# Hybrid decoder trunk on one core: query/key projections with 512 moving columns, distance tables on ScalarE and VectorE, and two dense pieces per step early in attention

## The chip, the cores and the metric

The kernel runs on one core of a Trainium2 chip. The metric is the device time of one execution in microseconds (us). Engines are named as the profile names them: PE is TensorE's matmul, PEld its weight load, DVE is VectorE, ACT is ScalarE, POOL is GpSimd, SP is SyncE (here it issues the weight DMAs).

## The reference

Two layers of a decoder trunk with 256 positions and width 1024, then a final RMS norm. Each layer normalises x, projects it with one wide matrix, runs three causal token mixers side by side, gates and sums them, and adds a SwiGLU feed-forward block:

```python
h = _rms_norm(x, attn_norm)
aq, ak, av, bq, bk, bv, c_q, c_kv_pe, gates = jnp.split(h @ w_in, offsets, axis=-1)
y_a = _diff_attention(aq, ak, av, ...) @ w_branch_a       # 4 heads x 2 maps of 64, distance slopes
y_b = _dilated_attention(bq, bk, bv, slopes_b) @ w_branch_b   # 4 heads of 128, three strides
y_c = _mla(c_q, c_kv_pe, ...) @ w_branch_c                # 8 heads, latent q and kv, rope
g_a, g_b, g_c = jnp.split(jax.nn.sigmoid(gates), 3, axis=-1)
x = x + (g_a * y_a + g_b * y_b + g_c * y_c) @ w_out
h2 = _rms_norm(x, ffn_norm)
x = x + (jax.nn.silu(h2 @ w_ffn_gate) * (h2 @ w_ffn_up)) @ w_ffn_down
```

All inputs are float32.

## The kernel before

**Numbers in two parts.** A float32 matrix is held as two tiles of the matmul type fp32r: `hi`, a copy rounded by ACT (`hi_of`, line 223), and `lo`, the rest, by a DVE subtraction (`lo_of`, lines 228 and 230). A product is the sum of three matmuls, hi with hi, hi with lo and lo with hi (`mm3`, lines 212 to 215).

**Weights.** `PLAN` lists every weight block in order of use, in pieces of up to 1024 columns a partition. `dma_piece` (line 242) loads a piece into one of 5 `raw` tiles; `split_piece` makes `whi` on ACT and `wlo` on DVE, 5 tiles of each. `take` (line 255) hands out the next piece and splits a later one, 3 pieces ahead.

**The dense stream.** `dense` (line 455) is a generator of one layer's projections, which yields after each weight piece: the latent projections (8 pieces), query/key of mixer a (`qk_proj`, 8), the latent up-projections (`mla_up`, 5), values of a (4), query/key of b (8), values of b (4), and then for each of the branches a, c, b in turn two times a gate (4) and a branch product (2). `pump(n)` draws n pieces. 25 pieces are drawn ahead of `attention`, and there `pump(1)` (line 936) draws one at the end of each of 22 steps; what is left is drawn after it. The steps run the scores, softmax, transposes, values and outputs of 16 heads (4 of a, 8 of c, 4 of b) at fixed lags. The order that is written here is not yet the order on the engines: the Tile framework schedules the instructions of each engine at build time by a timeline of its own (`schedule_with_timeline_sim`), and an instruction written earlier goes first where both are ready. Each engine then runs its own list strictly in order.

**Query/key projections.** `qk_proj` (lines 505 to 527) has four jobs j, two for queries and two for keys, each for 256 output columns. A job takes one PSUM bank of four (`N_DENSE`), and `pair_job` (lines 263 to 273) fills it over 8 row blocks k and 2 column blocks c with the weights stationary and the activations x[k] moving. The tile x[k] holds 256 columns of hi and, beside them, 256 columns of lo, and each of the three matmuls of `mm3` moves 256 columns. Then DVE multiplies the bank by the norm factor of each position (line 514 or 516), the bank is free, and the result t is split into hi and lo on ACT and DVE (`stacked` for mixer a, lines 495 to 502; lines 522 and 525 for b).

**Distance tables.** `tables` (lines 326 to 345), called once in layer 0, loads three constants and makes 8 tables of 128x256 on POOL: 4 for a (line 338), 4 for b with two instructions each (lines 342 and 343). The softmax reads them (line 757). POOL's other work is the rope (lines 602 to 605), the reciprocal roots (line 372) and the scaling of a's outputs (line 843).

**Tiles.** `PairRing` holds 16 tiles (`N_PAIR`) of 1024 columns for split activations; each is used whole or as two halves.

Of the kernel before, what the change touches and what calls it, by code (L numbers as in the profile page):

```python
# [12 lines left out]
F32 = mybir.dt.float32  # L13
F32R = mybir.dt.float32r
AF = mybir.ActivationFunctionType
ALU = mybir.AluOpType
# [13 lines left out]
SLOPE_A = [2.0 ** -(2 * h + 1) for h in range(4)]  # L30
SLOPE_B = [2.0 ** -(2 * h + 2) for h in range(4)]
SL = (slice(256, 384), slice(0, 256))
MASKED = 3.0e32
PIECE = 1024
N_PAIR = 16
N_F = 9
N_DENSE = 4
N_RAW = 5
N_PIECE = 5
AHEAD = 3  # L40
LAG_T, LAG_V, LAG_O, LAG_X = 3, 4, 6, 2
WARM = 10

C_ID, C_DM, C_DB, C_LC, C_TC, C_CS = 0, 128, 384, 640, 896, 1152
# [130 lines left out]
def fields(t):  # L175
    v = t.rearrange("p (c f t) -> p c f t", c=2, f=2)
    return v[:, :, 0], v[:, :, 1]


def split_rows(t):  # L180
    return t.rearrange("p (c t) -> p c t", c=2)


class Build:
    def __init__(self, nc, tc, ctx, x, xt, w, gains, lam, fnorm, cst, out):
# [6 lines left out]
        def ring(n, cols, dt, name, pool=cp):  # L192
            return Ring([pool.tile([128, cols], dt, name=f"{name}{i}") for i in range(n)])

        self.banks = ring(N_DENSE, 512, F32, "bank", pp)
        self.att = ring(8 - N_DENSE, 512, F32, "att", pp)
        self.fr = PairRing([cp.tile([128, 1024], F32R, name=f"fr{i}") for i in range(N_PAIR)])
        self.f = ring(N_F, 512, F32, "f")
# [26 lines left out]
    def lo_of(self, lo, src, hi, scale=None):  # L225
# [3 lines left out]
        else:  # L229
            self.nc.vector.scalar_tensor_tensor(out=lo, in0=src, scalar=scale, in1=h, op0=ALU.mult, op1=ALU.subtract)  # L230

    def split(self, hi, lo, src, scale=None):
        self.hi_of(hi, src, 1.0 if scale is None else scale)
        self.lo_of(lo, src, hi, scale)
# [26 lines left out]
        return [(self.whi[j][:, k * nc_:(k + 1) * nc_], self.wlo[j][:, k * nc_:(k + 1) * nc_]) for k in range(nk)]  # L261

    def pair_job(self, ps, x, nk):
        k = 0
        while k < nk:
            for wh, wl in self.take():
                for c in range(2):
                    s = slice(c * 128, c * 128 + 128)
                    self.mm3(ps[:, c * 256:c * 256 + 256], wh[:, s], wl[:, s], x[k][:, 0:256], x[k][:, 256:512],
                             k == 0 and c == 0, k == nk - 1)  # L270
                k += 1
            if k < nk:
                yield
# [15 lines left out]
    def setup(self):  # L289
# [19 lines left out]
        bank = self.banks.get()  # L309
        for _ in range(WARM):  # L310
            self.mm(bank[:, 0:128], self.ones, self.ones, True, True)
# [14 lines left out]
    def tables(self):  # L326
        nc, cp = self.nc, self.cp
        dm, db = self.f.get(), self.f.get()
        nc.sync.dma_start(out=dm[:, 0:256], in_=self.cst_in[:, C_DM:C_DM + 256])
        nc.sync.dma_start(out=db, in_=self.cst_in[:, C_DB:C_DB + 512])  # L330
        self.tc_c = cp.tile([128, 256], F32, name="tcc")
        nc.sync.dma_start(out=self.tc_c, in_=self.cst_in[:, C_TC:C_TC + 256])
        self.cs = cp.tile([128, 2, 2, 32], F32, name="cs")
        nc.sync.dma_start(out=self.cs, in_=self.cst_in[:, C_CS:C_CS + 128].rearrange("p (f b c) -> p f b c", f=2, b=2))
        self.ta, self.tb = [], []
        for h in range(4):
            t = cp.tile([128, 256], F32, name=f"ta{h}")
            nc.gpsimd.tensor_scalar(out=t, in0=dm[:, 0:256], scalar1=SLOPE_A[h], scalar2=None, op0=ALU.mult)
            self.ta.append(t)
        for h in range(4):  # L340
            t = cp.tile([128, 256], F32, name=f"tb{h}")
            nc.gpsimd.tensor_scalar(out=t, in0=db[:, 0:256], scalar1=SLOPE_B[h], scalar2=None, op0=ALU.mult)
            nc.gpsimd.tensor_tensor(out=t, in0=t, in1=db[:, 256:512], op=ALU.subtract)
            self.tb.append(t)
        self.f.put(dm, db)

# [136 lines left out]
        yield from self.branch(self.oc, False, False)  # L483
        yield from self.branch(self.ob, False, True)

    def key_pair(self, src, rows=slice(0, 128)):
        kd = self.fr.pair()
        self.split(*fields(kd[rows]), src)
        return kd

    def stacked(self, t, query, j):
# [13 lines left out]
    def qk_proj(self, q, k, scale, stacked):  # L505
        nc = self.nc
        for j in range(4):
            bank = self.banks.get()
            yield from self.pair_job(bank, self.xs, KT)
            ps = split_rows(bank)  # L510
            t = self.f.get()
            tv = split_rows(t)
            if j < 2:
                nc.vector.scalar_tensor_tensor(out=tv, in0=ps, scalar=-scale, in1=self.Rb, op0=ALU.mult, op1=ALU.mult)
            else:
                nc.vector.tensor_tensor(out=tv, in0=ps, in1=self.Rb, op=ALU.mult)  # L516
            self.banks.put(bank)
            if stacked:
                (q if j < 2 else k).append(self.stacked(t, j < 2, j))
            elif j < 2:  # L520
                hi, lo = self.fr.get(), self.fr.get()
                self.split(hi, lo, t)
                q.append((hi, lo))
            else:
                k.append(self.key_pair(tv))
            self.f.put(t)
            yield
# [391 lines left out]
    def attention(self, l, pump):  # L919
        self.pairs = {}  # L920
        units = [("a", h) for h in range(4)] + [("c", h) for h in range(8)] + [("b", h) for h in range(4)]
        stages = [self.unit_stages(kind, l, h) for kind, h in units]
        n = len(stages)

        def run(i, stage):
            if 0 <= i < n and stages[i][stage] is not None:
                stages[i][stage]()

        for s in range(n + LAG_O):
            run(s, 1)  # L930
            run(s - LAG_T, 3)
            run(s - LAG_V, 4)
            run(s - LAG_O, 5)
            run(s + LAG_X, 0)
            run(s, 2)
            pump(1)


    def out_proj(self, pairs, nk, g0, late):
# [212 lines left out]
```

## Time and profile before

| | |
|---|---|
| median of 3 runs | 884.61 us (883.76 to 885.02) |
| the profiled execution's own time | 883.18 us |
| its span, first to last instruction | 881.4 us |
| granted TensorE clock, share of full speed | 0.999 |
| PE busy | 873.6 us (99%), 4710 matmuls |
| DVE busy | 591.1 us (67%) |
| ACT busy | 502.2 us (57%) |
| POOL busy | 71.4 us (8%) |
| weights and inputs read | 154.03 MB, 176 GB/s over the span |

In the profile a line number such as L210 is that of the code above, and a helper's line stands for everything that calls it: all matmuls are L210, so they are told apart by their tiles. In `bank<-fr,whi` the tile `bank` is written, `fr` (activations) moves and `whi` (weights) is stationary, or the other way round in `bank<-whi,fr`. Matmuls are pipelined: a matmul's own duration includes its way through the array, and the next one starts long before it ends. What one costs is the distance from its start to the start of the next.

### The profile page before, as it was taken

To read this page: it belongs to the slowest core of one execution; us is meant where nothing else is said; L and a number is where in the kernel's file an instruction comes from. 1 tells how busy PE (TensorE), PEld (TensorE's weight loads), DVE (VectorE), ACT (ScalarE), POOL (GpSimd) and SP (SyncE) were. 2 spreads that over 40 slices of the span, in tenths; PEclk is the share of its full clock that TensorE was granted. 3 is DMA by queue.
4 is the path that set the end of the run, shared out by engine and by line. 5 is a ranking of instruction groups with operands and counts; after the bars stand their busy time and mean duration, and the time that the engine had idled before them with its cause. 6 is when DMAs were issued, how large, how long until landed. Compare 5 with 4: busy or idle time off the path is not lost.

```text
span 881.4 us, 12736 instructions
## 1 busy us (share of the span) xinstructions
PE 873.6 (99%) x4710; PEld 759.5 (86%) x4710; DVE 591.1 (67%) x990; ACT 502.2 (57%) x852; POOL 71.4 (8%) x95
## 2 busy tenths in 40 slices
PE   9999999999999999999999999999999999999997
PEld 9989988888888888888899899888888888888886
DVE  5988878665666655555467888786556666656444
ACT  7797777644454444444376867775454644444332
POOL 1940310000000000000011303100000000000000
PEclk9999999999999999999999999999999999999999
DMA  9756444456656665656475553444555556655541
GB/s 340 245 170 209 128 141 160 146 169 193 187 167 197 187 190 182 182 186 191 127 226 174 172 168 128 151 145 159 180 189 182 167 193 202 203 190 180 181 141 49
DMA packets 45423, 155.92 MB, mean 177 GB/s; under 512 B 5168, under 2 KB 6192, under 8 KB 45360
## 3 DMA queue, kind: packets, MB, share of 16 engines
q1 hardware_dynamic: 44928, 154.55, 55.0%
q8 instruction: 37, 0.61, 0.3%
q10 hardware_dynamic: 432, 0.55, 0.2%
q14 instruction: 26, 0.21, 0.1%
HBM read 154.03 MB, written 1.05 MB: 176 GB/s over the span
## 4 chain that ended last, share of the span: by engine, by line
PE 97%; POOL 1%; issue 1%; DVE 0%; ACT 0%; POOLq 0%
PE bank L210 87%; PE att L210 6%; PE att L445 2%; PE att L719 1%; PE att L767 0%; PE att L768 0%; PE att L769 0%; POOL f L602 0%; PE att L693 0%; PE att L851 0%; POOL f L604 0%; POOL f L603 0%; POOL q_tm L605 0%; DVE x_tm L1043 0%; ACT x_tm L1058 0%
## 5 line engine op out<-in xcount | busy, mean ns | idle before, releaser
L210 PE MATMUL bank<-whi,fr 128*128 128x512 f32 (+1 forms) x2032 | 631.1, 387 | 0.0
L228 DVE TENSOR_TENSOR wlo<-raw,whi 128x1024 fp32r<-128x1024 f32 (+2 forms) x294 | 353.9, 1206 | 250.8 <-ACT whi L223 250.1
L223 ACT ACTIVATE whi<-raw 128x1024 fp32r<-128x1024 f32 (+2 forms) x294 | 305.0, 1041 | 305.8 <-PE bank L210 246.0
L210 PEld LDWEIGHTS bank<-whi,fr 128*128 128x128 f32 x2032 | 379.8, 188 | 71.5 <-ACT whi L223 0.2
L210 PE MATMUL bank<-wlo,fr 128*128 128x512 f32 (+1 forms) x1016 | 390.1, 386 | 0.0
L210 PEld LDWEIGHTS bank<-wlo,fr 128*128 128x128 f32 x1016 | 191.0, 188 | 35.5 <-DVE wlo L228 0.3
L210 PE MATMUL bank<-fr,whi 128*128 128x256 f32 x512 | 94.6, 285 | 0.0
L210 PEld LDWEIGHTS bank<-fr,whi 128*128 128x128 f32 x512 | 80.0, 192 | 0.2
L210 PE MATMUL bank<-fr,wlo 128*128 128x256 f32 x256 | 73.0, 285 | 0.0
L210 PEld LDWEIGHTS bank<-fr,wlo 128*128 128x128 f32 x256 | 49.0, 192 | 0.0
L372 POOL TENSOR_TENSOR r<-small,mhalf 128x2 f32<-128x2 f32 x4 | 2.8, 708 | 477.5 <-DVE small L398 462.6
L759 ACT ACTIVATE s<-s,small 128x256 f32<-128x256 f32 (+1 forms) x80 | 35.8, 455 | 1.2 <-DVE small L757 0.8
L372 POOL TENSOR_TENSOR small<-small,mhalf 128x2 f32<-128x2 f32 (+1 forms) x12 | 10.0, 831 | 280.5 <-DVE small L1047 178.5
L223 ACT ACTIVATE fr<-att 128x512 fp32r<-128x512 f32 (+2 forms) x54 | 28.3, 559 | 4.1 <-PE att L719 2.3
L210 PE MATMUL att<-whi,fr 128*128 128x288 f32 (+1 forms) x108 | 29.9, 290 | 0.0
L228 DVE TENSOR_TENSOR fr<-att,fr 128x512 fp32r<-128x512 f32 (+2 forms) x46 | 28.2, 634 | 0.1
L223 ACT ACTIVATE fr<-f 64x512 fp32r<-64x512 f32 (+2 forms) x40 | 23.3, 583 | 6.7 <-DVE f L516 5.4
L210 PE MATMUL att<-fr,fr 96*128 96x256 f32 (+3 forms) x152 | 26.0, 277 | 0.0
L210 PEld LDWEIGHTS att<-fr,fr 96*128 96x128 f32 (+1 forms) x152 | 22.7, 190 | 0.6
L615 ACT ACTIVATE f<-bank,rh 128x512 f32<-128x512 f32 x24 | 16.3, 689 | 11.7 <-PE bank L210 11.7
L972 ACT ACTIVATE f<-bank,rh 128x512 f32<-128x512 f32 (+1 forms) x24 | 15.6, 654 | 12.2 <-PE bank L210 12.2
L210 PEld LDWEIGHTS att<-whi,fr 128*128 128x128 f32 x108 | 20.4, 191 | 0.1
(134 smaller groups left out, 636.0 us busy)
## 6 DMA issues: line engine op xcount, KB each, us to landing
raw<-w SPq DMA_DIRECT2D x272, 512.0 KB, 3.6
raw<-w SPq DMA_DIRECT2D x16, 336.0 KB, 3.2
raw<-w SPq DMA_DIRECT2D x6, 384.0 KB, 3.6
x_tm<-xt SPq DMA_DIRECT2D x2, 512.0 KB, 6.4
f<-x SPq DMA_DIRECT2D x3, 256.0 KB, 5.2
f<-fnorm SPq DMA_DIRECT2D x2, 256.0 KB, 4.2
out<-x_tm ACTq DMA_DIRECT2D x2, 256.0 KB, 2.2
f<-x SPq DMA_DIRECT2D x2, 128.0 KB, 3.1
```

What stands on the lines that cost most here:

```text
L210: self.nc.tensor.matmul(out, lhsT, rhs, start=start, stop=stop, skip_group_check=True)
L223: self.nc.scalar.activation(out=hi, in_=src, func=AF.Copy, scale=scale)
L228: self.nc.vector.tensor_tensor(out=lo, in0=src, in1=h, op=ALU.subtract)
L372: self.nc.gpsimd.tensor_tensor(out=out, in0=v, in1=self.mhalf[:, 0:v.shape[1]], op=ALU.pow)
L445: self.nc.tensor.transpose(ps[:, c, b * 128:b * 128 + 128], src[b][:, c0 + c * 128:c0 + c * 128 + 128], self.ident)
L615: nc.scalar.activation(out=t[b], in_=bank[b], func=AF.Tanh, scale=self.rh[:, b:b + 1])
L719: nc.tensor.transpose(ps[0:96, c, b * 128:b * 128 + 128], src[:, b, 2 * p + c, :], self.ident)
L759: nc.scalar.activation(out=s[:, SL[b]], in_=s[:, SL[b]], func=AF.Exp, bias=mn[:, b:b + 1], scale=-1.0, accum_out=z[:, b:b + 1])
L972: nc.scalar.activation(out=a, in_=g, func=AF.Tanh, scale=self.rh[:, b:b + 1])
```

## The change

The query/key job takes two banks, one for each column block c. The stationary hi weights meet hi and lo of x[k] in one matmul of 512 moving columns, and the lo weights meet hi in one of 256 as before. To empty a bank, ACT copies its right half (with the scale of the queries), DVE adds the left half to it, and after both banks POOL multiplies by the norm factor; then t is split as before. `key_pair` and line 522 are written out, with the same instructions (`lo_pool` and the argument `pool` are not used by any call). The tables are made by ACT (a) and by one DVE instruction each (b). `attention` draws two pieces in the steps 0 to 7. There are 18 tiles in place of 16 in `PairRing`, and the SBUF set aside for DMA descriptors is cut to 1024 bytes a partition; no DMA of the profile was issued from POOL.

```diff
-N_PAIR = 16
+N_PAIR = 18
...
+SLOW = 8
...
+    def lo_pool(self, lo, src, hi):
+        self.nc.gpsimd.tensor_tensor(out=lo, in0=src, in1=hi.bitcast(F32), op=ALU.subtract)
...
     def pair_job(self, ps, x, nk):
...
                 for c in range(2):
                     s = slice(c * 128, c * 128 + 128)
-                    self.mm3(ps[:, c * 256:c * 256 + 256], wh[:, s], wl[:, s], x[k][:, 0:256], x[k][:, 256:512],
-                             k == 0 and c == 0, k == nk - 1)
+                    self.mm(ps[c], wh[:, s], x[k], k == 0, False)
+                    self.mm(ps[c][:, 0:256], wl[:, s], x[k][:, 0:256], False, k == nk - 1)
...
-            nc.gpsimd.tensor_scalar(out=t, in0=dm[:, 0:256], scalar1=SLOPE_A[h], scalar2=None, op0=ALU.mult)
+            nc.scalar.activation(out=t, in_=dm[:, 0:256], func=AF.Copy, scale=SLOPE_A[h])
...
-            nc.gpsimd.tensor_scalar(out=t, in0=db[:, 0:256], scalar1=SLOPE_B[h], scalar2=None, op0=ALU.mult)
-            nc.gpsimd.tensor_tensor(out=t, in0=t, in1=db[:, 256:512], op=ALU.subtract)
+            nc.vector.scalar_tensor_tensor(out=t, in0=db[:, 0:256], scalar=SLOPE_B[h], in1=db[:, 256:512], op0=ALU.mult,
+                                           op1=ALU.subtract)
...
-    def key_pair(self, src, rows=slice(0, 128)):
+    def key_pair(self, src, rows=slice(0, 128), pool=False):
         kd = self.fr.pair()
-        self.split(*fields(kd[rows]), src)
+        hi, lo = fields(kd[rows])
+        self.hi_of(hi, src)
+        (self.lo_pool if pool else self.lo_of)(lo, src, hi)
         return kd
...
         for j in range(4):
-            bank = self.banks.get()
+            bank = [self.banks.get() for _ in range(2)]
             yield from self.pair_job(bank, self.xs, KT)
-            ps = split_rows(bank)
             t = self.f.get()
             tv = split_rows(t)
-            if j < 2:
-                nc.vector.scalar_tensor_tensor(out=tv, in0=ps, scalar=-scale, in1=self.Rb, op0=ALU.mult, op1=ALU.mult)
-            else:
-                nc.vector.tensor_tensor(out=tv, in0=ps, in1=self.Rb, op=ALU.mult)
-            self.banks.put(bank)
+            sign = -scale if j < 2 else 1.0
+            for c in range(2):
+                nc.scalar.activation(out=tv[:, c], in_=bank[c][:, 256:512], func=AF.Copy, scale=sign)
+                nc.vector.scalar_tensor_tensor(out=tv[:, c], in0=bank[c][:, 0:256], scalar=sign, in1=tv[:, c],
+                                               op0=ALU.mult, op1=ALU.add)
+            self.banks.put(*bank)
+            nc.gpsimd.tensor_tensor(out=tv, in0=tv, in1=self.Rb, op=ALU.mult)
             if stacked:
                 (q if j < 2 else k).append(self.stacked(t, j < 2, j))
             elif j < 2:
                 hi, lo = self.fr.get(), self.fr.get()
-                self.split(hi, lo, t)
+                self.hi_of(hi, t)
+                self.lo_of(lo, t, hi)
                 q.append((hi, lo))
...
-            pump(1)
+            pump(2 if s < SLOW else 1)
...
-    nc = bacc.Bacc("TRN2", target_bir_lowering=False, num_devices=1)
+    nc = bacc.Bacc("TRN2", target_bir_lowering=False, num_devices=1, dynamic_dma_scratch_size=1024)
```

## Rows read from the trace of the kernel before

**Rows 1.** The page: span, busy time, and the chain that ended last

```profile
span 881.4 us, 12736 instructions
...
PE 873.6 (99%) x4710; PEld 759.5 (86%) x4710; DVE 591.1 (67%) x990; ACT 502.2 (57%) x852; POOL 71.4 (8%) x95
...
PE 97%; POOL 1%; issue 1%; DVE 0%; ACT 0%; POOLq 0%
```

**Rows 2.** Timeline of PE, 25 to 46 us: start, us, line, count

```profile
25.58 0.40 PE L210 MATMUL bank<-fr,whi 128*128 128x256 f32 x2
...
45.26 0.28 PE L210 MATMUL bank<-fr,wlo 128*128 128x256 f32 x1
```

**Rows 3.** Timeline of PE, 178 to 220 us: start, us, line, count

```profile
178.27 0.67 PE L210 MATMUL bank<-whi,fr 128*128 128x512 f32 x2
...
219.16 0.39 PE L210 MATMUL bank<-whi,fr 128*128 128x512 f32 x1
```

**Rows 4.** Groups by line and shape, PE: count | busy us, mean ns | idle

```profile
L210 PE MATMUL bank<-fr,whi 128*128 128x256 f32 x512 | 94.6, 285 | 0.0
L210 PE MATMUL bank<-fr,wlo 128*128 128x256 f32 x256 | 73.0, 285 | 0.0
```

**Rows 5.** Timeline, 59 to 61 us: the wait of the query transposes

```profile
59.78 0.28 PE L719 MATMUL att<-ident,q_tm 128*96 128x128 f32 x1
59.83 0.73 POOL L605 TENSOR_TENSOR q_tm<-f,f 128x256 f32<-128x256 f32 x1
...
60.62 0.54 PE L719 MATMUL att<-ident,q_tm 128*96 128x128 f32 x3 [0.55 <-POOL q_tm L605]
```

**Rows 6.** Groups by line and shape: what the new instructions resemble

```profile
L514 DVE SCALAR_TENSOR_TENSOR f<-bank,row 128x512 f32<-128x512 f32 x8 | 5.5, 687 | 2.0 <-PE bank L210 1.9
L588 ACT ACTIVATE k_tm<-bank,rk 128x256 f32<-128x256 f32 x8 | 3.9, 485 | 0.0
L230 DVE SCALAR_TENSOR_TENSOR fr<-att,gains,fr 128x256 fp32r<-128x256 f32 x34 | 14.6, 477 | 0.4 <-ACT fr L223 0.3
```

**Rows 7.** Timeline of POOL: tables (24 and 29 us), query rope (53 and 56)

```profile
24.23 4.49 POOL L338 TENSOR_SCALAR ta<-f 128x256 f32<-128x256 f32 x4
...
29.06 5.47 POOL L342 TENSOR_SCALAR tb<-f 128x256 f32<-128x256 f32 x4
...
52.86 0.75 POOL L602 TENSOR_TENSOR f<-q_tm,cs 128x256 f32<-128x256 f32 x1 [6.92 <-ACT q_tm L563]
...
56.21 1.72 POOL L602 TENSOR_TENSOR f<-q_tm,cs 128x256 f32<-128x256 f32 x1
```

**Rows 8.** Busy us (count) in stretches: PE, PEld, DVE, ACT, POOL; clock, DMA

```profile
21.00:33.00 12.00, 12.00 (x103) 11.97 (x102) 9.85 (x23) 12.00 (x28) 9.47 (x12) 1.00 0.80 279
33.00:45.30 12.30, 12.30 (x105) 12.30 (x104) 12.08 (x14) 5.69 (x10) 12.30 (x15) 1.00 0.69 225
45.30:60.00 14.70, 14.70 (x87) 13.62 (x86) 12.44 (x27) 14.54 (x29) 7.62 (x9) 1.00 0.57 174
60.00:80.00 20.00, 19.45 (x120) 17.50 (x120) 17.89 (x42) 15.66 (x35) 0.56 (x1) 1.00 0.66 210
80.00:100.00 20.00, 20.00 (x174) 20.00 (x173) 18.44 (x57) 15.21 (x40) 1.90 (x3) 1.00 0.50 143
456.00:470.00 14.00, 14.00 (x120) 14.00 (x119) 11.12 (x18) 11.33 (x25) 5.41 (x14) 1.00 0.60 187
470.00:482.00 12.00, 12.00 (x99) 12.00 (x98) 8.10 (x11) 7.81 (x11) 0.00 (x0) 1.00 0.49 161
```

**Rows 9.** Timeline of ACT, 39 to 45 us: a wait for DVE

```profile
39.02 0.85 ACT L223 ACTIVATE whi<-raw 128x768 fp32r<-128x768 f32 x1 [0.74 <-ACT fr L223]
44.60 0.64 ACT L223 ACTIVATE fr<-f 64x512 fp32r<-64x512 f32 x1 [4.73 <-DVE f L516]
```

**Rows 10.** Timeline of DVE: a weight split beside POOL, and one without

```profile
57.47 1.55 DVE L228 TENSOR_TENSOR wlo<-raw,whi 128x1024 fp32r<-128x1024 f32 x1
...
65.69 1.21 DVE L228 TENSOR_TENSOR wlo<-raw,whi 128x1024 fp32r<-128x1024 f32 x1
```

## The prediction

> **What bounds the kernel now.** I read the page first: PE is busy 99% of the span, and the chain that ended last is PE for 97% of it [rows 1]. A busy share is not yet a bound, because the matmuls overlap, so the next view is PE's timeline, where the distance between starts is the cost. In the first query/key projections 164 steps of 256 columns lie between 25.58 and 45.26 us: 19.68 us / 164 = 120.0 ns each [rows 2]. In a long stretch of 512 columns 180 steps take 40.89 us: 227.2 ns each [rows 3]. Both run without a break; PE is the bound through its own rate and not through waits. The one wait of PE that I found after the start-up, over 0.3 us, is at 60 us, where a transpose waits for POOL's rope of the queries: 0.84 us between the starts [rows 5]. A matmul of 128 columns costs at most the 0.12 us of 256, so 0.7 us are lost there. The last view is the busy time by stretch: around the first projections ACT and DVE are nearly full [rows 8]. That is where a change that gives them work can hurt.
>
> **Part 1, the matmuls.** There are 512 matmuls with the hi weights and 256 with the lo weights in the query/key jobs [rows 4], that is 256 triples of 3 x 120.0 = 360.0 ns. After the change each is one of 512 and one of 256 columns: 227.2 + 120.0 = 347.2 ns. The moved columns stay 768. The gain is 12.8 ns x 256 = **3.3 us**, all of it on PE's path, which nothing covers. Both prices come from steady stretches, so its bounds are close: 2.8 to 3.6 us (2 ns either way on a triple, an estimate from the last digits of the rows).
>
> A rule of the Trainium skill speaks against this size. "TensorE: Matmul & The Clock Gate", section "Back-to-back issue gap", prices a single warm matmul at its columns over 2.4 GHz plus about 2.5 ns; by that a matmul less saves 2.5 ns, and 256 of them 0.6 us. The rows do not agree: twice 120.0 less 227.2 is 12.8 ns per matmul. I take the rows; the other case is rival C.
>
> **Part 2, emptying the banks.** Now DVE needs 0.69 us a job (row L514) and the bank is free. Afterwards a job needs two ACT copies of 128x256 from PSUM (like L588, 0.49 each) and two DVE instructions (like L230, 0.48 each) [rows 6], then one POOL product of 128x512. POOL has no row of that size; from the rope rows a two-input 128x256 takes 0.75 us with DVE idle and 1.72 beside it [rows 7], so twice that, 1.5 to 3.4 us. I take 2.5, the middle, since DVE is busy 70 to 98% there [rows 8]. Per projection of four jobs: ACT +3.9, DVE 3.8 - 2.8 = +1.1, POOL +10 us. The bank is free some 1.5 us after the last matmul in place of 0.7, and a job fills for 16 x 0.347 = 5.6 us, so with two pairs of banks the next but one finds its pair empty. The latent up-projection behind the last job wants all four banks, but reaches the second pair only after six matmuls, and can run its first half ahead. I cost the banks at nothing; with that cover gone it would be about 1 us at each of two such places.
>
> What waits longer is t: its hi copies on ACT now stand behind POOL. ACT runs in order, so weight splits are queued behind a copy that waits, then DVE's lo parts, then PE. The splits run some pieces ahead (8 triples are 2.9 us). The trace shows the cover: at 39.87 us ACT waited 4.73 us for DVE's product of the same chain [rows 9], and PE ran on at 120 ns all through [rows 2].
>
> **Part 3, the tables.** POOL loses 8 instructions on rows and 4 more (24 to 43 us; 4.49 + 5.47 us for the first eight [rows 7]). ACT gets four (0.49 x 4 = 1.9, priced as L588) and DVE four (0.48 x 4 = 1.9). The tables are read only from the first softmax on, so these have room to be moved. Two things improve besides: POOL reaches the rope and roots earlier, and DVE's splits lose a neighbour (1.55 beside POOL, 1.21 alone [rows 10]); but the four products put some 10 us of POOL work back. I cost both at nothing.
>
> **ACT and DVE around the first projections.** Over 21 to 60 us (39.0 us) ACT is busy 12.00 + 5.69 + 14.54 = 32.2 and DVE 9.85 + 12.08 + 12.44 = 34.4 [rows 8]. Added are 3.9 + 1.9 = 5.8 and 1.1 + 1.9 = 3.0: 38.0 and 37.4 of 39. It fits, barely. The cost of new waits lies between 0 (all fits, as the sum says) and 5.8 us (none of ACT's idle time can be used). I take **0.7 us**: the nearest row is the ACT wait of 4.73 us that cost nothing, and one short wait like that of rows 5 is what such a tight stretch shows now. In layer 1 there are no tables, and from 456 to 482 us ACT idles 6.9 us of 26 and DVE 6.8 [rows 8]; no cost. A waits' gain below zero would be the 0.7 of rows 5, which comes next.
>
> **Part 4, two pieces per step.** The eight extra pieces are the same matmuls, weight DMAs and splits, written earlier; SP's queue keeps its order. They stand between the query rope and the transposes that wait for it [rows 5] and give PE 2 x 2.8 us more to do, so I take that wait of **0.7 us** as gone (between 0 and 0.7). In the attention of b's projections DVE is at 90% (36.3 of 40 us from 60 to 100 [rows 8]); a dense piece needs 1.2 us of DVE for 2.8 of PE, so more of them in these steps thin DVE's load. New is that the second half of branch a is now written in steps 8 and 9, right behind the last output of a, instead of steps 16 and 17. If PE stood there for the split of that output it would be about 1 us a layer (an ACT and a DVE instruction of 0.48 each); later gates and scores of c are ready to fill in, so I cost it at nothing. The two more tiles, the smaller scratch and the rewritten `key_pair` cost nothing: no instruction changes.
>
> **Sum** against the profiled execution (883.18 us, span 881.4): -3.3 - 0.7 + 0.7 = -3.3, so 879.9. The median of the runs stands 1.4 above that execution, so the median after should be 884.6 - 3.3 = **881.3 us**.
>
> **Rivals.**
> A, ACT and DVE overflow in layer 0: the added 5.8 us find half of the idle time, PE waits 3 us in all between 45 and 65 us; 884.6 - 4.0 + 3.0 = **883.6**. For it: 38.0 of 39 us. Against it: rows 9.
> B, slower: ACT's hi copies stand at the head of its queue waiting for POOL, in all four jobs of layer 0, at POOL's long price of 3.4 us, 13.6 in all. ACT has 1.0 us idle left, and 4.7 were shown to be covered once; 7.9 remain for PE: 884.6 - 4.0 + 7.9 = **888.5**. It decides the sign from 9.7 us of such waits, 2.4 a job. For it: POOL is slowest when DVE is full, as it is here. Against it: the instructions' order is planned with POOL's times, and a copy can be set behind splits.
> C, the matmul saving isn't there, by the rule above or because a price of 227 holds only with other operands: -0.6 - 0.7 + 0.7 gives **884.0**. Against it: both prices are steady over 160 steps and more.
>
> **How the numbers follow.** Forecast 0.66, A 0.14, B 0.12, C 0.08. A measurement of this kernel tells 0.2% (1.8 us) from no change. The forecast is faster, as is 0.02 of A (its waits under 2 us); the rest of A and C are within 0.2%; B is slower: 0.68, 0.20, 0.12. The forecast's own range is 880.0 (no new wait, and the banks and rope as taken, with the larger saving) to 882.3 (new waits of 1.7). The range reaches over A and C to 885.0 and, for the runs' own spread of 0.8 below the median, down to 879.4; B is left out.
>
> **What would show it.** Right: 512 matmuls of the query/key jobs, 256 of each width, at 227 and 120 ns; no wait of PE over 0.3 us at 60 us; ACT and DVE over 95% busy from 21 to 60 us with PE unbroken. Wrong: PE gaps between 45 and 65 us that end on ACT's `whi` or DVE's `wlo` (A); ACT waits for POOL's product of 2.4 us or more with PE idle behind them (B); unequal steps, 120 and 240 ns (C); or gaps at the outputs of a or at the banks, which I cost at nothing.

## The result and the profile after

The changed kernel is slower. Its median is 890.0 us over six runs (888.25 to 891.1), beside 883.77 us for the kernel before in the runs next to it: a ratio of 1.0067 [1.0055, 1.0079]. The profiled execution took 889.9 us. Forecast were 881.3 us, a gain of 3.3; it came out 6.2 us the other way.

In the code after the change the line numbers have moved: matmuls are L211, hi parts L224, lo parts L229, the copies of the projected queries L572, the rope L611 to L614, the transposes of head pairs L728. New are the emptying of a bank, L521 (ACT) and L522 (DVE), and POOL's product L525.

The page of the kernel after, to be read beside [rows 1] (span, busy time, the chain that ended last) and, in its last three lines, beside [rows 4, 6] (groups by line):

```profile
span 888.1 us, 12276 instructions
...
PE 875.9 (99%) x4454; PEld 746.7 (84%) x4454; DVE 596.2 (67%) x1010; ACT 512.2 (58%) x888; POOL 70.5 (8%) x99
...
PE 94%; ACT 2%; DVE 1%; issue 1%; POOL 1%; DMA 1%; SPq 0%; POOLq 0%; ACTq 0%; DVEq 0%
...
L211 PE MATMUL bank<-fr,whi 128*128 128x512 f32 x256 | 90.7, 400 | 0.5 <-DVE f L522 0.5
L211 PE MATMUL bank<-fr,wlo 128*128 128x256 f32 x256 | 70.6, 281 | 0.0
...
L525 POOL TENSOR_TENSOR f<-f,row 128x512 f32<-128x512 f32 x16 | 23.1, 1445 | 92.9 <-DVE f L522 89.4
```

The change did what its text says: 256 matmuls fewer, and half of those left in the query/key jobs are 512 columns wide. PE is still the bound at 99%, but its share of the last chain fell from 97 to 94%, and ACT, DVE and POOL now stand in that chain. PE does less and waits more. The waits view tells for whom (engine and tile, awaited engine and tile: us in total, times, longest); the last line is ACT's own wait for the new product.

```profile
PE att L728 <- POOL q_tm L614: 3.4, 2, 1.7
PE bank L211 <- DVE ones L309: 1.0, 1, 1.0
PE att L211 <- DVE small L766: 0.6, 1, 0.6
PE bank L211 <- DVE f L522: 0.5, 1, 0.5
PE bank L211 <- ACT q_tm L572: 0.3, 1, 0.3
...
ACT fr L224 <- POOL f L525: 4.9, 7, 2.2
```

The first line is the wait of [rows 5], the query transposes for the rope. Before, it came once and showed 0.55 us; now it comes twice, once in each layer, at 1.7 us. The second line is the start-up. Three stretches of the kernel after (columns as in rows 8) show the two places and what happened after the first:

```profile
60.00:64.00 4.00, 2.29 (x14) 1.89 (x14) 4.00 (x11) 4.00 (x11) 3.48 (x4) 1.00 0.59 154
64.00:68.00 4.00, 3.28 (x14) 2.48 (x12) 4.00 (x13) 4.00 (x10) 0.00 (x0) 0.65 0.70 244
...
498.00:504.00 6.00, 4.33 (x25) 3.43 (x24) 5.96 (x18) 6.00 (x17) 4.16 (x4) 1.00 0.58 197
```

PE is busy 2.29 of 4.00 us from 60 us and 4.33 of 6.00 from 498; POOL, busy 0.56 and 0.00 us there before, is busy 3.48 and 4.16. In the second stretch the granted clock is 0.65 of full speed in the mean, so PE ran a good part of it at the lower of its two levels (1.2 GHz in place of 2.4), after it had stood at 61.7 to 63.6 us and again, shorter, at 65 us. From 65.5 to 68.6 us the granted clock is 0.50, and the matmuls there lost some 1.6 us by it. Five of the six executions have a mean granted clock of 0.996 and took 889.7 to 891.1 us; the sixth has 0.998 and took 888.25.

**Where the time went.** Between the first and the last start of a matmul lie 873.9 us before and 880.6 after: +6.7. Worked out from the distances between starts in the timeline: the new matmuls gave back 1.7 us (below). Layer 0 lost 4.5 us between 60 and 70 us (1.88 at the query transposes, 0.73 at 65.5 us, some 1.6 by the lower clock, the rest small waits) and 0.5 at 59.3, where PE waited for ACT to copy out a bank; layer 1 lost 1.84 us at 500.8, a bank was awaited for 0.6 us at 34 us, and the start-up took 0.6 more. Against this stand the 1.7 us and the 0.7 that the kernel before had lost at its own transposes [rows 5]. That is 8.0 - 1.7 - 0.7 = 5.6 of the 6.7; the remaining 1.1 is spread out.

**Why the rope is late.** The timeline of the kernel after (start, us), first layer 0, then the matmuls' own price, then the last query/key job of layer 1 and what follows it:

```profile
59.22 0.56 ACT L572 ACTIVATE q_tm<-bank,rq 128x384 f32<-128x384 f32 x1
...
61.62 0.27 PE L211 MATMUL att<-low,fr 128*128 128x128 f32 x1
...
62.77 0.79 POOL L614 TENSOR_TENSOR q_tm<-f,f 128x256 f32<-128x256 f32 x1
...
63.61 0.53 PE L728 MATMUL att<-ident,q_tm 128*96 128x128 f32 x3 [1.71 <-POOL q_tm L614]
...
65.51 0.58 PE L211 MATMUL att<-fr,fr 128*128 128x256 f32 x1 [0.57 <-DVE small L766]
...
471.32 0.40 PE L211 MATMUL bank<-fr,whi 128*128 128x512 f32 x1
471.56 0.28 PE L211 MATMUL bank<-fr,wlo 128*128 128x256 f32 x1
...
477.68 0.40 PE L211 MATMUL bank<-fr,whi 128*128 128x512 f32 x1
...
480.15 0.63 PE L211 MATMUL bank<-fr,whi 128*128 128x512 f32 x2
480.62 0.28 PE L211 MATMUL bank<-fr,wlo 128*128 128x256 f32 x1
...
484.23 2.60 ACT L224 ACTIVATE fr<-f 64x512 fp32r<-64x512 f32 x4 [0.83 <-POOL f L525]
484.97 0.28 PE L211 MATMUL bank<-fr,wlo 128*128 128x256 f32 x1
485.09 0.34 PE L211 MATMUL bank<-whi,fr 128*128 128x384 f32 x1
486.74 0.36 ACT L521 ACTIVATE f<-bank 128x256 f32<-128x256 f32 x1
487.12 1.06 ACT L224 ACTIVATE whi<-raw 128x1024 fp32r<-128x1024 f32 x1
487.13 0.42 DVE L522 SCALAR_TENSOR_TENSOR f<-bank,f 128x256 f32<-128x256 f32 x1 [0.53 <-ACT f L521]
488.09 0.36 ACT L521 ACTIVATE f<-bank 128x256 f32<-128x256 f32 x1
488.35 1.04 ACT L572 ACTIVATE q_tm<-bank,rq 128x384 f32<-128x384 f32 x2
489.36 0.42 DVE L522 SCALAR_TENSOR_TENSOR f<-bank,f 128x256 f32<-128x256 f32 x1
489.57 0.39 PE L211 MATMUL bank<-whi,fr 128*128 128x384 f32 x1
...
497.79 0.56 ACT L572 ACTIVATE q_tm<-bank,rq 128x384 f32<-128x384 f32 x1
498.43 0.75 POOL L611 TENSOR_TENSOR f<-q_tm,cs 128x256 f32<-128x256 f32 x1 [4.85 <-ACT q_tm L572]
...
500.77 0.28 PE L728 MATMUL att<-ident,k_tm 128*96 128x128 f32 x1
501.08 1.59 POOL L614 TENSOR_TENSOR q_tm<-f,f 128x256 f32<-128x256 f32 x1
...
502.72 0.53 PE L728 MATMUL att<-ident,q_tm 128*96 128x128 f32 x3 [1.67 <-POOL q_tm L614]
```

The last matmul of the job starts at 484.97, and the first 18 matmuls of the queries' up-projection (384 columns) go at once into the two banks that were free. ACT, however, has begun at 484.23 the four hi copies of the job before, after a wait for POOL's product; a copy that empties a bank comes at 486.74, a weight split at 487.12, the copy for the second bank at 488.09, and DVE's sum is done at 489.78. So that bank comes free 4.8 us after the last matmul. The second row block of the up-projection starts at 489.57 and is cut in two (9 matmuls, then 9 from 492.48). Before, all 36 ran in a row from 480.43. PE stands for neither bank here: the first is free at 487.56, the second at 489.78, and the two parts start 2.0 and 2.7 us later, at the places that the order planned at build time gives them. That the plan cuts the block because the banks come free late fits e9 and e12 below; the plan's own times are not in the trace. The second block's last copy on ACT comes at 497.79, 9.0 us after the first block's last; then POOL's rope (498.43 to 502.67), and PE, whose order is fixed, stands at 500.77 before the transposes of these queries. The late bank is not all of this delay. The second block's last matmul starts at 493.89, 3.9 us ahead of that copy, and in layer 0 at 54.09, 5.1 us ahead of the copy at 59.22; in both layers the copy stands in ACT's queue behind hi copies, softmax instructions and weight splits.

The matmuls: from 471.32 to 477.68 lie 18 pairs of one 512 and one 256, 353.3 ns each, some 236 ns from a 512 to what follows and some 117 from a 256. At 480.15 two of the 512s follow each other directly, and they take 0.47 us, again some 235 ns each. Two lines of the kernel before, beside [rows 3], show 512s of the other kind, whose weights move; here a 256 stands behind them:

```profile
58.47 0.62 PE L210 MATMUL bank<-whi,fr 128*128 128x512 f32 x2
58.92 0.28 PE L210 MATMUL att<-fr,fr 128*128 128x256 f32 x1
```

These two take 0.45 us, some 226 ns each, like the long run of [rows 3].

### The profile page after: what moved, and what is told of

The parts are those of the page before. It is cut to its first block, busy times and chain, and to the rows that moved or that the text cites. A ratio compares the mean times of both kernels' runs of the same rounds, so it can differ in the third digit from the quotient of the medians.

```text
span 888.1 us, 12276 instructions
## 1 busy us (share of the span) xinstructions
PE 875.9 (99%) x4454; PEld 746.7 (84%) x4454; DVE 596.2 (67%) x1010; ACT 512.2 (58%) x888; POOL 70.5 (8%) x99
## 4 chain that ended last, share of the span: by engine, by line
PE 94%; ACT 2%; DVE 1%; issue 1%; POOL 1%; DMA 1%; SPq 0%; POOLq 0%; ACTq 0%; DVEq 0%
PE bank L211 84%; PE att L211 6%; PE att L450 2%; ACT fr L224 1%; PE att L728 1%; DMA f<-x 1%; ACT whi L224 1%; ACT s L768 0%; DVE wlo L229 0%; PE att L776 0%; PE att L778 0%; PE att L777 0%; POOL f L525 0%; PE att L702 0%; PE att L860 0%
## 5 line engine op out<-in xcount | busy, mean ns | idle before, releaser
L211 PE MATMUL bank<-whi,fr 128*128 128x512 f32 (+1 forms) x2032 | 636.0, 388 | 0.4 <-ACT q_tm L572 0.3
L229 DVE TENSOR_TENSOR wlo<-raw,whi 128x1024 fp32r<-128x1024 f32 (+2 forms) x294 | 354.6, 1208 | 238.2 <-ACT whi L224 237.1
L224 ACT ACTIVATE whi<-raw 128x1024 fp32r<-128x1024 f32 (+2 forms) x294 | 305.1, 1041 | 281.6 <-PE bank L211 226.7
L211 PEld LDWEIGHTS bank<-whi,fr 128*128 128x128 f32 x2032 | 380.7, 188 | 72.5 <-ACT q_tm L572 0.8
L211 PE MATMUL bank<-wlo,fr 128*128 128x512 f32 (+1 forms) x1016 | 391.4, 387 | 0.0
L211 PEld LDWEIGHTS bank<-wlo,fr 128*128 128x128 f32 x1016 | 191.4, 188 | 35.2 <-DVE wlo L229 0.3
L211 PE MATMUL bank<-fr,whi 128*128 128x512 f32 x256 | 90.7, 400 | 0.5 <-DVE f L522 0.5
L211 PE MATMUL bank<-fr,wlo 128*128 128x256 f32 x256 | 70.6, 281 | 0.0
L211 PEld LDWEIGHTS bank<-fr,whi 128*128 128x128 f32 x256 | 47.5, 188 | 11.3 <-DVE f L522 0.8
L211 PEld LDWEIGHTS bank<-fr,wlo 128*128 128x128 f32 x256 | 48.2, 189 | 0.7
L224 ACT ACTIVATE fr<-att 128x512 fp32r<-128x512 f32 (+2 forms) x54 | 28.5, 559 | 7.2 <-PE att L211 3.8
L229 DVE TENSOR_TENSOR fr<-att,fr 128x512 fp32r<-128x512 f32 (+2 forms) x46 | 28.2, 635 | 3.6 <-ACT fr L224 3.3
L525 POOL TENSOR_TENSOR f<-f,row 128x512 f32<-128x512 f32 x16 | 23.1, 1445 | 92.9 <-DVE f L522 89.4
L211 PE MATMUL att<-whi,fr 128*128 128x288 f32 (+1 forms) x108 | 30.1, 292 | 0.0
L377 POOL TENSOR_TENSOR small<-small,mhalf 128x2 f32<-128x2 f32 (+1 forms) x12 | 8.2, 687 | 231.6 <-DVE small L1056 178.5
L224 ACT ACTIVATE fr<-f 64x512 fp32r<-64x512 f32 (+2 forms) x40 | 23.3, 583 | 5.4 <-POOL f L525 4.9
L211 PE MATMUL att<-fr,fr 96*128 96x256 f32 (+3 forms) x152 | 25.5, 277 | 0.6 <-DVE small L766 0.6
L211 PEld LDWEIGHTS att<-fr,fr 96*128 96x128 f32 (+1 forms) x152 | 22.8, 191 | 2.1 <-DVE small L766 0.8
```

Of the source, the lines that this page charges most:

```text
L211: self.nc.tensor.matmul(out, lhsT, rhs, start=start, stop=stop, skip_group_check=True)
L224: self.nc.scalar.activation(out=hi, in_=src, func=AF.Copy, scale=scale)
L229: self.nc.vector.tensor_tensor(out=lo, in0=src, in1=h, op=ALU.subtract)
L377: self.nc.gpsimd.tensor_tensor(out=out, in0=v, in1=self.mhalf[:, 0:v.shape[1]], op=ALU.pow)
L525: nc.gpsimd.tensor_tensor(out=tv, in0=tv, in1=self.Rb, op=ALU.mult)
```

## The experiments

Two theories stood. One is that of the banks, BANKS in the expectations: two of four banks are held and come free late, so the up-projection is split and the rope late. The other is the new product on POOL, behind which ACT's hi copies, and all else in ACT's queue, stand. The first four runs come ahead of these and ask which part of the change costs; their theories 1 to 3 are spelled out in the expectation of e1. All kernels compute the whole reference. Each edit also lets the framework plan the order on the engines anew, so that a run can differ from its base in more than the lines edited (e9 shows how much). Each ratio is to the kernel before in runs on the same chip (medians 883.76 to 883.9 us).

**e1, e2, e3: one part alone.** e1 is the changed kernel with the tables back on POOL and one piece per step, so that the 512-column jobs are left (with the 18 tiles and the smaller scratch). e2 is the kernel before with two pieces per step, 18 tiles and the smaller scratch. e3 is the kernel before with the tables on ACT and DVE.

```diff
 e1, against the kernel after
-            nc.scalar.activation(out=t, in_=dm[:, 0:256], func=AF.Copy, scale=SLOPE_A[h])
+            nc.gpsimd.tensor_scalar(out=t, in0=dm[:, 0:256], scalar1=SLOPE_A[h], scalar2=None, op0=ALU.mult)
...
-            pump(2 if s < SLOW else 1)
+            pump(1)
```

> The 512-column jobs with their new emptying alone: tables on POOL and one piece per step as before. Theory 1 (the loss is PE standing at the query transposes for the rope, because the longer emptying chain on ACT, DVE and POOL makes the rope late; in the changed kernel 1.9 us at 61.6 us, 1.8 us at 500.8 us, and a stretch at half clock after the first): these waits stay, 886 to 890 us. Theory 2 (the second piece per step puts weight splits ahead of the rope on ACT and DVE) and theory 3 (the tables fill ACT and DVE): the 3.3 us of the matmuls come through, 880 to 882 us.

> Two pieces per step in the first eight steps alone (with 18 tiles and the smaller scratch), all else as before. Theory 1: no long wait is new, 883 to 885 us. Theory 2: waits of 1.5 us or more at the query transposes in both layers, 886 to 890 us. Theory 3: 883 to 885 us.

> The distance tables on ACT and DVE alone, all else as before. Theory 3: PE waits between 30 and 66 us, 886 us or more. Theories 1 and 2: 883 to 885 us, at best the 0.7 us wait at 60 us gone.

e1: 889.11 us, 1.0068 [1.0056, 1.0081]. e2: 884.55, 1.0008 [1.0000, 1.0017]. e3: 883.2, 0.9994 [0.9986, 1.0003]. The jobs alone carry the loss (5.4 us of it by the medians, the ratio as large); the other two parts cost and bring nothing that can be told. The waits view of PE in e1 has the same wait at the transposes, and one for a hi copy on ACT:

```profile
PE att L728 <- POOL q_tm L614: 3.0, 2, 1.7
PE att L211 <- ACT fr L224: 2.0, 1, 2.0
```

**e4: the changed kernel with one piece per step** (`pump(1)`). It asks whether the second piece covers the rope, as the prediction had it.

> The changed kernel with one piece per step throughout. Theory 2: the long waits at the query transposes go in both layers, 881 to 884 us. Theory 1: they stay, 887 to 891 us. Theory 3: the waits in layer 0 stay and those of layer 1 go, 885 to 888 us.

890.89 us, 1.0084 [1.0071, 1.0098]. The wait at the transposes stands (3.3 us, twice, longest 1.7), so the second piece doesn't touch it. In the profiled execution the clock stayed whole after it; it took 888.17 us, while the four others, with a mean granted clock of 0.992 to 0.995, took 890.8 to 891.9. The same stretch as above:

```profile
64.00:68.00 4.00, 3.27 (x19) 2.42 (x18) 4.00 (x13) 4.00 (x10) 0.00 (x0) 1.00 0.72 237
```

**e5: e1 with the product on DVE.**

```diff
-            nc.gpsimd.tensor_tensor(out=tv, in0=tv, in1=self.Rb, op=ALU.mult)
+            nc.vector.tensor_tensor(out=tv, in0=tv, in1=self.Rb, op=ALU.mult)
```

> The 512-column jobs alone (as in e1_cols_only), but the product by the norm factor on DVE in place of POOL. Theory POOL (the product on POOL makes t late and stands ahead of the rope): the waits of 1.5 to 2 us at the query transposes go, 881 to 884 us. Theory BANKS (the last job of mixer a holds two of the four banks while they are emptied, so the up-projection's second row block, which needs them, its copy on ACT and its rope come late): they stay within 1 us, 886 to 890 us.

886.58 us, 1.0030 [1.0019, 1.0040]: 2.5 us better than e1 and still 2.8 over the kernel before. The wait at the transposes is down to 0.3 us. The up-projection is still cut, but its second block starts at 486.46, where in e1 it starts at 488.95:

```profile
486.46 0.39 PE L211 MATMUL bank<-whi,fr 128*128 128x384 f32 x1
```

POOL is one part of the loss and not the whole.

**e6: e1, and the last job of mixer a the old way,** in one bank with three matmuls of 256 columns, emptied by DVE alone; the up-projection then finds three free banks.

```diff
-            bank = [self.banks.get() for _ in range(2)]
-            yield from self.pair_job(bank, self.xs, KT)
+            one = stacked and j == 3
+            bank = self.banks.get() if one else [self.banks.get() for _ in range(2)]
+            yield from self.pair_job(bank, self.xs, KT, one)
...
```

> The 512-column jobs alone, but the last of the four jobs of mixer a done as before, in one bank with three matmuls of 256 columns and one product on DVE. Theory BANKS: the up-projection runs in one piece, the waits at the query transposes shrink to 1 us or less in both layers, 881.5 to 884 us (matmul saving 3.3 x 14/16 = 2.9 us). Theory POOL: the three other products stay on POOL, the waits shrink by less than half, 886 us or more.

885.19 us, 1.0016 [1.0007, 1.0025]: one job of four taken back returns 3.9 us of e1's loss. The up-projection is now cut 27 to 9, with 0.24 us between, and layer 1 has no wait; in layer 0 some 3 us remain, for banks, for splits and 0.9 at the query transposes. The time lies between the ranges of the two theories. The place behind the last job is where most of the loss arises; since this edit takes away the job's second bank, its ACT copies and its POOL product at once, it doesn't tell these apart.

**e7, e8: the column blocks in turn.** A job fills one bank over all eight k, then the next, and each half is emptied and multiplied by itself, so that a half is out of the way early. e8 is e7 with the tables on ACT and DVE.

```diff
-            for wh, wl in self.take():
-                for c in range(2):
...
+                self.pair_step(ps, 0, wh, wl, x, len(w), nk)
+                w.append((wh, wl))
...
+        done(0, ps)
+        ps = self.banks.get()
+        for k, (wh, wl) in enumerate(w):
+            self.pair_step(ps, 1, wh, wl, x, k, nk)
+        done(1, ps)
```

> The 512-column jobs alone, with the column blocks in turn: block 0 over all eight row blocks in one bank, then block 1 in the next, so that the first bank is emptied beside the second half; the POOL product is made in halves. The same matmuls as in e1_cols_only. Theory BANKS: only one bank is still to be emptied when the up-projection begins, the waits at the query transposes shrink to 1 us or less, 880.5 to 884 us. Theory POOL: they stay, 886 us or more.

> As e7_turn, with the tables on ACT and DVE too. Theory BANKS: as e7_turn or up to 0.7 us less, 880 to 884 us. If the tables fill ACT and DVE where the jobs are emptied, layer 0 has new waits and it is 2 us or more above e7_turn.

890.22 us, 1.0070 [1.0057, 1.0084], and 889.86, 1.0061 [1.0048, 1.0073]: misses. The emptying copies stood in ACT's queue behind hi copies that waited for POOL, four times and 4.0 us at the longest, so that even with a single bank to empty PE waited for it (waits and, last, timeline of e7; this execution took 892.76 us, the longest of five):

```profile
PE bank L211 <- DVE f L527: 1.9, 1, 1.9
...
ACT fr L224 <- POOL f L530: 5.9, 4, 4.0
...
51.51 0.44 PE L211 MATMUL bank<-whi,fr 128*128 128x384 f32 x1 [1.86 <-DVE f L527]
```

How many banks are held is thus not the point by itself; what stands ahead of the emptying in the queue has a part in it.

**e9: the kernel after, with banks of its own for the second row block.** That block of the up-projection takes two banks of the attention's pool, so it needn't wait for the jobs' banks. The emptying and POOL stay as they are.

```diff
-        pu = [[self.banks.get() for _ in range(2)] for _ in range(2)]
+        own = [self.banks, self.att]
+        pu = [[own[b].get() for _ in range(2)] for b in range(2)]
...
-                self.banks.put(pu[b][f])
+                own[b].put(pu[b][f])
```

> The changed kernel, with the up-projection's second row block in two of the four attention banks in place of the two that the last query/key job must first empty. Theory BANKS: the up-projection of the queries is not split, its rope comes some 5 us earlier, the waits of 1.9 and 1.8 us at the query transposes and the half clock behind the first go: 882.5 to 885.5 us. Theory POOL: they stay, 888 us or more.

884.23 us, 1.0006 [0.9997, 1.0015]: 5.8 us of the loss are gone. The second block is not cut any more (in layer 1, 33 of the 36 matmuls run in a row from 481.96 and three had run ahead; in layer 0, 30 in a row from 47.20), and no transpose waits. The emptying on ACT is about as slow as ever: the last job's second bank is free at 486.21, 4.4 us after its last matmul at 481.84. The second block's copies (line 573 here) come in one go, 4.3 us after the first's (timeline of e9: the copies and the end of the rope in layer 1, then the end of the rope and the transposes, line 729 here, in layer 0):

```profile
486.81 1.03 ACT L573 ACTIVATE q_tm<-bank,rq 128x384 f32<-128x384 f32 x2
...
491.14 1.05 ACT L573 ACTIVATE q_tm<-att,rq 128x384 f32<-128x384 f32 x2
...
495.35 0.74 POOL L615 TENSOR_TENSOR q_tm<-f,f 128x256 f32<-128x256 f32 x1
...
61.86 1.42 POOL L615 TENSOR_TENSOR q_tm<-f,f 128x256 f32<-128x256 f32 x2
...
66.47 0.60 PE L729 MATMUL att<-ident,q_tm 128*96 128x128 f32 x4
```

In layer 1 the rope ends at 496.10 in place of 502.67, so that PE would not have waited even at the old place of the transposes. In layer 0 it ends at 63.28, hardly ahead of the 63.55 of the kernel after. There the wait is gone because the new plan puts dense matmuls on PE from 62.21 on and the transposes only at 66.47 (in layer 1 they moved too, to 518.10). So e9 shows what the edit is worth, and for layer 1 that the rope comes earlier; that banks alone, with PE's order as it was, would have saved layer 0 is not shown.

**e10: the kernel after, the transposes one step later** (`LAG_X` 1 in place of 2), which would hide a late rope.

> The changed kernel, with the head pairs of mixer c made one step later (LAG_X 1 in place of 2), so that the query transposes are written a step, some 5 us of PE work, further back. Banks and POOL as in the changed kernel. If the place of the transposes in PE's fixed order is what turns a late rope into lost time (both theories): the waits at the transposes go, 883 to 886 us, though the rope is as late. If PE lacks other work there: 888 us or more.

890.74 us, 1.0078 [1.0066, 1.0091]: a miss. The wait for the rope is there once instead of twice: in layer 1 the transposes stand where they stood. In layer 0 they come later, at 65.40, but PE stands in place of the rope for DVE's work on the softmax (waits of PE in e10):

```profile
PE att L776 <- DVE s L821: 2.0, 1, 2.0
PE att L728 <- POOL q_tm L614: 1.5, 1, 1.5
```

**e11: e9 with e5's edit,** both suspects gone.

> As e9_own_banks, and the product by the norm factor on DVE in place of POOL. Theory BANKS: within 1 us of e9_own_banks. Theory POOL: 2 us or more below it.

882.16 us, 0.9984 [0.9975, 0.9993]: 1.7 us below the kernel before, and its interval is clear of 1. Of PE's waits there remain 0.5 and 0.3 us beside the start-up. The edit of the banks is worth 5.8 us (after to e9); the product's move is worth 2.1 behind it (e9 to e11) and 2.5 without it (e1 to e5), so the two hardly overlap.

**e12: the kernel before, each job holding a second, unused bank.** Does holding two cost anything when the emptying is short?

```diff
-            bank = self.banks.get()
+            bank, spare = self.banks.get(), self.banks.get()
...
-            self.banks.put(bank)
+            self.banks.put(bank, spare)
```

> The kernel before, with each query/key job holding a second bank that it does not use, until the first is emptied by the one DVE product; nothing else is changed. Theory BANKS in its plain form (two banks held are enough): new waits at the query transposes, 885 to 888 us. If the longer emptying on ACT and DVE is needed too: 883 to 885 us.

883.95 us, 1.0001 [0.9992, 1.0009], with the up-projection uncut (36 matmuls from 481.34). The plain form of the theory, that two held banks are too many, falls. It takes the longer emptying or POOL's product too.

**e13: the kernel after, both emptying instructions on DVE,** so that no emptying stands in ACT's queue.

```diff
-                nc.scalar.activation(out=tv[:, c], in_=bank[c][:, 256:512], func=AF.Copy, scale=sign)
+                nc.vector.tensor_scalar(out=tv[:, c], in0=bank[c][:, 256:512], scalar1=sign, scalar2=None, op0=ALU.mult)
```

> The changed kernel, with the copy of each bank's right half on DVE in place of ACT; the product stays on POOL. If the banks are late because the copies stand in ACT's queue behind hi copies that wait for POOL: the second bank is free within 3 us of the job's end in place of 4.8, the waits at the query transposes shrink to under 1 us each, 883 to 886 us. If the emptying is too long on any engine, or DVE is too full: 887 us or more.

889.24 us, 1.0057 [1.0043, 1.0071]: a miss. The banks did come free early: the sums for the last job of layer 1 were done at 485.24, 2.2 us after the up-projection's start at 483.03, and it is cut only once, 18 and 18 with 1.0 us between. But ACT still stood behind POOL, and the copies of the queries with it (timeline of ACT in e13):

```profile
481.59 2.60 ACT L224 ACTIVATE fr<-f 64x512 fp32r<-64x512 f32 x4 [2.06 <-POOL f L525]
486.19 0.58 ACT L572 ACTIVATE q_tm<-bank,rq 128x384 f32<-128x384 f32 x1
487.72 2.60 ACT L224 ACTIVATE fr<-f 64x512 fp32r<-64x512 f32 x4 [0.95 <-POOL f L525]
...
494.48 1.03 ACT L572 ACTIVATE q_tm<-bank,rq 128x384 f32<-128x384 f32 x2
```

So freeing the jobs' banks early on DVE does not do what separate banks did in e9. The copies of the queries, which free the up-projection's own banks, were spread over 8.3 us here (486.19 to 494.48), and PE waited for them (1.2 us in two waits) as well as for a sum on DVE (1.7) and the rope (1.0). DVE had more to do, too, and POOL's product took 1.82 us in the mean, in place of 1.45. Which of these keeps e13 as slow as it is was not told apart.

**e14, e15: e11 without the rest of the change.** e14 draws one piece per step, e15 has the tables on POOL as well, so only the 512-column jobs, the own banks and the product on DVE are left (with the 18 tiles and the smaller scratch).

> e11_own_banks_dve with one piece per step. If the second piece covers waits: 883.5 us or more. If it does nothing: 881.5 to 882.8 us.

> e14_own_dve_one_piece with the tables on POOL as before: the 512-column jobs alone, their product on DVE, the up-projection in its own banks. If the tables beside cost or gain nothing: within 0.7 us of e14. If the POOL tables slow the rope or DVE: 0.7 us or more above it.

Both 882.32 us: 0.9981 [0.9972, 0.9990] and 0.9980 [0.9971, 0.9989]. The second piece and the tables bring nothing even with the waits gone. What is left brings 883.84 - 882.32 = 1.5 us, near the 1.7 of the timeline. It is not the matmuls alone: the wait of [rows 5] is gone as well (0.7), and e15 has new waits of 0.7 and 0.4 us. The kernel before with own banks was not run.

## Why the prediction was wrong, point by point

**What bounds the kernel: right.** PE's path sets the end before and after, and every loss is time that PE stood or ran at the lower clock.

**Part 1, the matmuls: the mechanism right, the term of 3.3 us twice too large.** Taken were 227.2 + 120.0 = 347.2 ns a pair. Measured were 353.3: the gain is 6.7 ns, not 12.8, and 256 of them give 1.7 us, not 3.3. The 256 costs some 117 ns, but from the start of a 512 to that of the 256 behind it pass some 236 ns, not 227. The price of 227 was read from 512s whose weights move [rows 3]; in the new ones the activations move. In the lines above, the new 512 costs as much with another 512 behind it, and the old kind costs no more with a 256 behind it. So the change of widths alone does not explain the surplus; whether it comes with the operand that moves, with the one that is stationary or with their order was not tried. The rule of the Trainium skill that was weighed ("TensorE: Matmul & The Clock Gate", section "Back-to-back issue gap") would have given, as an estimate, 2.5 ns a matmul, 0.6 us in all; the trace shows neither. Rival C comes near on this point: it named a price of 227 that "holds only with other operands", and its sign, steps of 120 and 240 ns, is close to the 117 and 236 found. Its saving of 0.6 us is too small, though, and its time of 884.0 us leaves no room for the new waits.

**Part 2, emptying the banks: the step that failed.** "The bank is free some 1.5 us after the last matmul" added up the durations of the instructions; in layer 1 the second bank was free after 4.8 us. The copies took less than their price (0.36 us, where 0.49 were taken), but they stood in ACT's queue behind four hi copies (2.60 us), which had waited for POOL, and behind a weight split (1.06). "I cost the banks at nothing; with that cover gone it would be about 1 us at each of two such places": the prediction named the stage (the up-projection wants all four banks) and the fallback, and took the cover as given because the first half could run ahead. It did run ahead. What was not followed is the second half: whose copy it delays, and that the rope behind this copy was already the latest thing in layer 0 [rows 5]. That wait had no slack to give; in layer 1 the rope had ended 1.4 us ahead of its transposes (493.47 and 494.84 before), less than it was delayed. PE stood 1.9 us in each layer, and in layer 0 further waits and a stretch at the lower clock came on top, 4.5 us in all. e9 returns 5.8 us. For layer 1 it shows that with the block uncut the rope ends in time; in layer 0 the rope ends as late, and the order on PE changed instead, so the way from the banks to that wait stays open.

POOL's product took 1.45 us in the mean, just under the lower bound of 1.5 and far from the 2.5 that was taken for DVE's being busy. Thirteen of the sixteen took 1.29 to 1.31 us, two of them with DVE at work on the softmax all through; the three longer ones, 1.95 to 2.27, each ran beside a weight split on DVE. Dear is less its duration than its place between instructions of other engines: ACT's ordered queue passes its wait on, and on POOL the rope stands behind it. e5 and e11 put the move to DVE at 2.1 to 2.5 us; which of the two ways carries it was not told apart.

**The one term for new waits, 0.7 us** with bounds of 0 and 5.8, was worked out from busy time and offset by the 0.7 of rows 5, so that waits came to nothing in the sum. Measured from the first to the last matmul, waits and the lower clock took 6.7 + 1.7 = 8.4 us more than before.

**The cover read from rows 9** did hold where it was read: the weight splits ran ahead, and PE lost nothing to them there. But ACT's queue also held the emptying copies and the copies of the queries, for which nothing runs ahead.

**Part 3, the tables: right,** nothing within what can be told (e3; e14 to e15). **"In layer 1 ... no cost"** failed: busy shares with 6.9 us of idle time on ACT said that there was room, but not in which order the queue would use it; 1.84 us were lost there.

**Part 4, two pieces per step: the work itself free, as costed; its gain did not come.** The wait of rows 5 did not go but grew from 0.7 to 1.9 us, and a second one came. The pieces between the rope and the transposes did not make up for a rope that ends 3.0 us later in layer 0 (63.55 in place of 60.56), and e4 has the same wait without them. On the kernel before, e2 has 0.2 us left of that wait and no gain in time; e3, which only moved the tables, has none of it left and no gain that can be told either.

**The rivals.** B named the right sign, nearly the right time (888.5 against 890.0) and a part of the mechanism, ACT's copies at the head of its queue waiting for POOL. That its time is so near is luck, since its place and its price were others: PE starved of weight splits in layer 0 alone, by a product of 3.4 us. Its condition, 2.4 us of such waits a job, was not met: ACT shows 4.9 us of them in all, 2.2 at the longest. PE did not wait for splits; it waited for the rope in both layers and for banks in layer 0. A's overflow is not what costs: the tables' extra work changes nothing (e1 loses as much without it), and e9 carries the same work on ACT and DVE and has the loss gone.

## What to carry to other kernels

When a cheaper form of matmul takes more PSUM banks, or a longer way to empty them, don't add up the durations of the new instructions: put each into the ordered queue that it shares and read off when the bank comes free. Then look past the next job for the stage that wants the most banks at once, and follow its last piece to the tightest wait that the trace already shows; a wait that shows at all has no slack. Take the price of a matmul from a stretch with the same moving and stationary operands, or keep the whole difference as an uncertainty. And where a framework plans the order anew for each edit, compare the order in both traces before an experiment's gain is put down to the edited lines.

## What was not expected of the hardware

- A pair of one 512- and one 256-column matmul with moving activations costs 353.3 ns, 6.1 more than the sum of the two steady prices (227.2 + 120.0). A 512 with moving activations takes some 235 ns also where another 512 follows it (480.15), one with moving weights some 226 also where a 256 follows (58.47, before). What causes the surplus was not tried.
- After PE had stood 1.9 us, and 0.6 us once more, the granted clock was 0.50 from 65.5 to 68.6 us; after like waits in e4's profiled execution it stayed 1.00. What tells the two apart is not shown here.
- POOL's product of 128x512 took from 1.29 us (layer 1, after) to 2.31 us (e13); the same product on DVE took 0.68 to 0.72 in the mean (e11, e5), with less than 0.2 us of waits before it in all.
